# Where the compressed branch's scores and turned weights live in PSUM: a two-layer NSA and GLA trunk on one core

## The chip, the core and the metric

The kernel runs on one core of one Trainium2 chip. Its five engines are TensorE (PE, with its weight loads shown apart as PEld), VectorE (DVE), ScalarE (ACT), GpSimd (POOL) and SyncE (SP), which issues the transfers. The metric is the device time of one execution in microseconds (us), the median over several runs.

## The reference

The reference runs two layers over a sequence of 512 rows of width 1024. In each layer a normalised input is projected by one wide matrix; from the parts two branches are made, a sparse attention of eight heads in two groups and a gated linear attention, which are mixed by gates and projected back. The part that matters here is the attention of one head. It has three branches over the same queries: compressed keys (31 of them, of blocks of 32 rows), selected blocks, and a window.

```
def _masked_softmax(s, mask):
    s = jnp.where(mask, s.astype(jnp.float32), -jnp.inf)
    m = jnp.max(s, axis=-1, keepdims=True)
    ...
    return e / jnp.maximum(jnp.sum(e, axis=-1, keepdims=True), 1e-30)

s_c = jnp.einsum('bqghd,bgjd->bghqj', qn, k_cmp) * scale
p_c = _masked_softmax(s_c, cmp_end[None, :] <= t[:, None])
o_c = jnp.einsum('bghqj,bgjd->bqghd', p_c.astype(v_cmp.dtype), v_cmp)
...
o_s = jnp.einsum('bghqkl,bgqkld->bqghd', p_s.astype(v_sel.dtype), v_sel)
...
o_w = jnp.einsum('bghqk,bkgd->bqghd', p_w.astype(vwin.dtype), vwin)
return gt[..., 0:1] * o_c + gt[..., 1:2] * o_s + gt[..., 2:3] * o_w
```

With 512 rows there are eight blocks, so all blocks are selected and the window spans the sequence; selection and window differ in their keys and values alone.

## The kernel before

The work of a layer is laid out by hand for TensorE; for the other engines the order comes from a scheduler, and each engine runs its instructions in that order. Accumulators live in the eight banks of PSUM, given out by four pools: three banks `mm` for the projections, two `s` and two `t` for scores and transposes, one `o` for the attention's output (line 84). A bank is given again when its last reader on VectorE or ScalarE is through. The program fixes at build time which bank each tile gets.

A projection (`fm`, L164) takes one bank of `mm` and fills it in eight steps of three matmuls (`split3`, L160 to L162), each 128 by 512: a weight is split into a high and a low part, and so are the activations. Its epilogue on ScalarE and VectorE (for instance L436 and L438, or L595) reads the bank. The weights come by DMA into `raw`; ScalarE casts the high part (L145) and VectorE subtracts it for the low part (L146).

During the attention the projections still to be done wait in a queue. `fill(us)` works off as many projection steps as the credit given allows; `need(name)` works until a certain one is done. So the projections fill the gaps of the attention steps on TensorE, which would have nothing to do while VectorE and ScalarE do a softmax.

The attention goes over four pairs of heads p (0 to 3, here also called the first to the fourth pair). Each pair has five steps in the list `steps`: one compressed step and four steps `attn_steps`, for two halves of the queries (ip) times two branches (br). Each is a generator, and `go(n)` carries step n to its next `yield`. The compressed step, `cmp_steps`, has three stages. First the scores: a mask and four small matmuls into one bank (L733, L736), read by VectorE at L740 (the extreme) and L743 (the difference), then exponent, sum, and the scaled weights at L751. Then the turn: four transposes (L755) into one bank, read by ScalarE (L757) and VectorE (L758). Last the product with the values (L761, L762) into the bank `o`, in which the attention steps accumulate theirs (L841) until VectorE reads it at L846.

An attention step makes scores for two blocks of 128 queries. A unit is one such call of `scores`: two matmuls into one bank for each of two head groups (L800), two banks in all, both of one pool, `s` or `t` by turns. VectorE masks them and finds the extreme (L813), ScalarE takes the exponent (L815), VectorE scales (L817, L818) and transposes in blocks of 32 (L778); over DRAM (L783, L786) they come back as `PT` for L841.

The loop that sets the order on TensorE goes over the twenty steps, with m the place in a pair and four gaps of projections for each:

```
for n in range(len(steps)):
    m = n % 5
    f4 = FILL[m]
    ...
    go(n)
    ...
    fill(f4[0])
    if m == 1:
        go(n - 1)
    fill(f4[1])
```

At m = 1 `go(n - 1)` is the turn of the same pair.

Of the kernel before, what the change touches and what calls it, by code (L numbers as in the profile page):

```python
# [64 lines left out]
def trunk(ctx, tc, x, wpk, sp, gvec, cs, wa, out):  # L65
# [23 lines left out]
    def new(pl, shape=(128, 512), dt=F32, tag=None, bufs=None):  # L89
        cnt[0] += 1  # L90
        kw = {} if bufs is None else {"bufs": bufs}
        return sb[pl].tile(list(shape), dt, tag=tag or pl, name=f"{tag or pl}_{cnt[0]}", **kw)

    def ps(tag):
        cnt[0] += 1
        return psp[tag].tile([128, 512], F32, tag=tag, name=f"ps_{tag}_{cnt[0]}")
# [4 lines left out]
    mm, tp = nc.tensor.matmul, nc.tensor.transpose  # L101
# [169 lines left out]
    for l in range(L):  # L271
# [20 lines left out]
        def fill(us):  # L292
            credit[0] += us
            while credit[0] > 0.3 and queue:
                credit[0] -= step(*queue[0])
# [9 lines left out]
        def need(name):  # L305
            while name not in done:
                step(*queue[0])
# [421 lines left out]

        def cmp_steps(p):  # L730
            qn = PR[p][0]
            c = ps("s")[:, 0:256]
            mm(c, ident_b, pmask.rearrange("p i g j -> p (i g j)"), start=True, stop=False,  # L733
               skip_group_check=True)
            for i in range(4):
                mm(c[:, i * 64:(i + 1) * 64], qn[:, i * 128:(i + 1) * 128], kbd, start=False, stop=True,  # L736
                   skip_group_check=True)
            c3 = c.rearrange("p (a j) -> p a j", j=32)
            mx = new("sm", (128, 8), tag="mx8")
            V.tensor_reduce(mx, c3, axis=X, op=OP.min)  # L740
            pc = new("g")
            pc3 = pc[:, 0:256].rearrange("p (a j) -> p a j", j=32)
            V.tensor_sub(pc3, mx.unsqueeze(2).to_broadcast([128, 8, 32]), c3)  # L743
            A.activation(pc[:, 0:256], pc[:, 0:256], AF.Exp)
            sm = new("sm", (128, 8), tag="sm8")
            V.tensor_reduce(sm, pc3, axis=X, op=OP.add)
            rc = new("sm", (128, 4, 2), tag="rc8")
            V.reciprocal(sm, sm)
            V.tensor_mul(rc, gt[:, :, 3 * p:3 * p + 13:12], sm.rearrange("p (i g) -> p i g", g=2))
            V.tensor_scalar(rc[:, 0], rc[:, 0], valid, None, op0=OP.mult)  # L750
            V.tensor_mul(pc3, pc3, rc.rearrange("p i g -> p (i g)").unsqueeze(2).to_broadcast([128, 8, 32]))  # L751
            yield
            bk = ps("t")
            for i in range(4):
                tp(bk[0:64, i * 128:(i + 1) * 128], pc[:, i * 64:(i + 1) * 64], ident)  # L755
            pcT = new("p", dt=F32R)
            A.copy(pcT[0:64], bk[0:64])  # L757
            V.tensor_sub(pcT[64:128], bk[0:64], pcT[0:64].bitcast(F32))  # L758
            yield
            acc = PR[p][3] = ps("o")  # L760
            mm(acc, vbd[0], pcT, start=True, stop=False, skip_group_check=True)  # L761
            mm(acc, vbd[1], pcT, start=False, stop=False, skip_group_check=True)  # L762
            yield
# [90 lines left out]
        for p in range(4):  # L854
            steps.append((p, cmp_steps, ()))
            steps += [(p, attn_steps, (ip, br)) for ip in range(2) for br in range(2)]
        live = [f(p, *a) for p, f, a in steps]

        def go(n):
            if 0 <= n < len(steps):  # L860
                next(live[n])
# [19 lines left out]
# [3 lines that stand above are left out]
            if m == 0:  # L884
                need(f"q{steps[n][0]}")
            if m == 4:
                need(f"nz{steps[n][0]}")
            go(n)
            if m == 3:
                go(n - 5)  # L890
                go(n - 4)
            fill(f4[0])
            if m == 1:
                go(n - 1)
            fill(f4[1])
            if m != 0:
                go(n)
                fill(f4[2])
            if m == 3:
                go(n - 3)  # L900
            if m == 4:
                go(n - 3)
                go(n - 2)
            fill(f4[3])
# [126 lines left out]
```

## Time and profile before

| | us |
|---|---|
| median of 3 runs | 830.52 (827.52 to 830.93) |
| profiled execution | 832.5, span 830.4 |
| TensorE busy | 790.9, 95% of the span |
| VectorE busy | 557.5, 67% |
| ScalarE busy | 354.4, 43% |
| GpSimd busy | 99.5, 12% |
| granted TensorE clock, mean | 0.993 |

Busy time is the time in which an engine had an instruction in work, without the instructions that only wait or issue. Shares are over the whole span, and stages differ: what an engine waits for has to be looked up in the stage in question. Start times are from the span's start. The attention of the first layer runs from about 150 to 320 us, that of the second from about 553 to 723 us.

### The profile page before, as it was taken

Reading aid. Unit: us, or ns where it says so; the run is one execution under the profiler, and the core shown is the slowest. Engines: PE = TensorE matmul, PEld = TensorE weight load, DVE = VectorE, ACT = ScalarE, POOL = GpSimd, SP = SyncE. Lnnn points to the kernel's source line nnn. Section 1 sums busy time; section 2 is a strip of 40 time slices with the busy share of each in tenths; the row PEclk is TensorE's granted clock in tenths of the full one; section 3 lists DMA queues with packets and bytes.
Section 4 is the critical chain, followed back from the end, with each engine's and each line's share of the span. In section 5 each row is a group of like instructions: output and inputs, shape, how many; then the busy total and the mean of one; then the engine's idle time right before and its main releaser. Section 6 shows DMA issues by size and latency. Waiting matters only on the chain. (4 is left out here: it accounts for less than half of the span.)

```text
span 830.4 us, 12007 instructions
## 1 busy us (share of the span) xinstructions
PE 790.9 (95%) x4250; PEld 648.0 (78%) x4250; DVE 557.5 (67%) x1272; ACT 354.4 (43%) x727; POOL 99.5 (12%) x118
## 2 busy tenths in 40 slices
PE   3999999998989999999999999999898999999996
PEld 3888788786868787888888878887776787778886
DVE  5653749898978863655564366589988888356322
ACT  3591136554444433443256413555544544344211
POOL 3100023000001002221010001321000100022100
PEclk9999999999999999999999999999999999999999
DMA  8432214367476575556246112234756666745222
GB/s 289 158 125 77 69 55 123 110 189 211 144 224 214 180 226 143 161 166 214 77 140 216 52 55 73 79 112 145 219 183 201 198 190 208 205 141 168 85 102 76
DMA packets 54555, 124.55 MB, mean 150 GB/s; under 512 B 6592, under 2 KB 23520, under 8 KB 54496
## 3 DMA queue, kind: packets, MB, share of 16 engines
q1 hardware_dynamic: 54496, 123.79, 47.6%
q8 instruction: 33, 0.54, 0.3%
q14 instruction: 26, 0.21, 0.1%
HBM read 95.46 MB, written 25.17 MB: 145 GB/s over the span
## 5 line engine op out<-in xcount | busy, mean ns | idle before, releaser
L160 PE MATMUL ps_mm<-hT,hl 128*128 128x512 f32 x544 | 219.1, 403 | 0.0
L161 PE MATMUL ps_mm<-hT,hl 128*128 128x512 f32 x544 | 213.9, 393 | 0.0
L162 PE MATMUL ps_mm<-hT,hl 128*128 128x512 f32 x544 | 213.5, 392 | 0.0
L145 ACT CAST hl<-raw 128x1024 fp32r<-128x1024 f32 (+3 forms) x110 | 100.4, 915 | 159.7 <-PE ps_mm L161 104.5
L146 DVE TENSOR_TENSOR hl<-raw,hl 128x1024 fp32r<-128x1024 f32 (+3 forms) x109 | 119.5, 1098 | 52.5 <-ACT hl L145 43.6
L160 PEld LDWEIGHTS ps_mm<-hT,hl 128*128 128x128 f32 x544 | 103.4, 190 | 23.3 <-issue 3.1
L162 PEld LDWEIGHTS ps_mm<-hT,hl 128*128 128x128 f32 x544 | 103.1, 190 | 22.5
L161 PEld LDWEIGHTS ps_mm<-hT,hl 128*128 128x128 f32 x544 | 103.5, 190 | 19.3
L815 ACT ACTIVATE g<-g,sx 128x128 f32<-128x128 f32 (+3 forms) x128 | 71.3, 558 | 80.3 <-DVE sx L813 71.6
L778 DVE STREAM_TRANSPOSE T<-g 128x256 f32<-128x256 f32 (+3 forms) x128 | 58.9, 492 | 0.7
L818 DVE TENSOR_SCALAR g<-g,sx,gt 128x128 f32<-128x128 f32 (+3 forms) x128 | 58.3, 469 | 1.5
L161 PE MATMUL ps_mm<-oT,hl 128*128 128x512 f32 x128 | 50.3, 393 | 1.7 <-POOL oT L849 1.7
L160 PE MATMUL ps_mm<-oT,hl 128*128 128x512 f32 x128 | 50.9, 397 | 0.0
L162 PE MATMUL ps_mm<-oT,hl 128*128 128x512 f32 x128 | 49.8, 389 | 0.0
L849 POOL TENSOR_TENSOR oT<-p,oT 128x512 fp32r<-128x512 f32 x8 | 13.6, 1696 | 254.6 <-ACT oT L848 254.6
L841 PE MATMUL ps_o<-PT,a 128*64 128x256 f32 (+1 forms) x384 | 38.6, 348 | 1.8 <-DMA PT<-tp 1.8
L183 POOL TENSOR_TENSOR rs<-ms,mhalf 128x1 f32<-128x1 f32 (+1 forms) x24 | 18.0, 751 | 174.3 <-DVE ms L181 170.6
L869 POOL TENSOR_TENSOR p<-p,g 128x512 f32<-128x512 f32 x16 | 28.0, 1753 | 84.2 <-DVE p L868 72.7
L841 PEld LDWEIGHTS ps_o<-PT,a 128*64 128x64 f32 x384 | 25.4, 137 | 16.2 <-issue 6.8
L813 DVE CUSTOM_DVE_ANT_0 g<-ps_s,cmask 128x128 f32<-128x128 f32 (+3 forms) x64 | 29.2, 485 | 9.1 <-PE ps_s L800 9.1
L800 PE MATMUL ps_t<-a,a 128*128 128x256 f32 (+2 forms) x112 | 25.1, 337 | 9.1 <-DVE p L758 4.7
L162 PE MATMUL ps_mm<-hl,hT 128*128 128x296 f32 (+1 forms) x96 | 32.4, 338 | 1.4 <-DVE hT L213 1.4
(253 smaller groups left out, 1323.7 us busy)
## 6 DMA issues: line engine op xcount, KB each, us to landing
raw<-wpk SPq DMA_DIRECT2D x96, 512.0 KB, 3.8
tp<-T SPq DMA_DIRECT2D x16, 896.0 KB, 4.1
PT<-tp SPq DMA_DIRECT2D x64, 224.0 KB, 5.2
raw<-wpk SPq DMA_DIRECT2D x32, 256.0 KB, 3.0
tp<-T SPq DMA_DIRECT2D x16, 384.0 KB, 2.4
PT<-tp SPq DMA_DIRECT2D x64, 96.0 KB, 2.7
a<-wpk SPq DMA_DIRECT2D x16, 256.0 KB, 4.7
p<-x SPq DMA_DIRECT2D x16, 256.0 KB, 2.8
```

Of the source, the lines that this page charges most:

```text
L145: A.copy(H[:, :w], r[:, :w])
L146: (G if i == 1 else V).tensor_tensor(Lo[:, :w], r[:, :w], H[:, :w].bitcast(F32), op=OP.subtract)
L160: mm(o, w[0], h[0], start=first, stop=False)
L161: mm(o, w[0], h[1], start=False, stop=False)
L162: mm(o, w[1], h[0], start=False, stop=last)
L778: V.transpose(t[:, :, :, g], pps[g][:, :n * 128].rearrange("p (j b q) -> p b j q", j=n, b=4))
L800: mm(o[g][:, :ww], PR[p][1][g][:, i * 128:(i + 1) * 128], kn, start=(n == 0), stop=(n == 1))
L813: V.tensor_tensor_reduce(pp[:, :w], ob, cmask[:, 512 - w:512], 1.0, -3 * NEG, OP.add, OP.min, sx[:, 0:1])
L815: A.activation(pp[:, :w], pp[:, :w], AF.Exp, bias=sx[:, 0:1], scale=-1.0, accum_out=sx[:, 1:2])
L818: V.tensor_scalar(pp[:, :w], pp[:, :w], sx[:, 2:3], gt[:, i, h * 3 + 1 + br:h * 3 + 2 + br], op0=OP.mult, op1=OP.mult)
L841: mm(acc[g * 64:(g + 1) * 64, (i0 + 2) * 128 - w:(i0 + 2) * 128], vsw[j // 2][:, j % 2, c0:c0 + 64], m, start=False, stop=(br == 1 and j = ...
L869: G.tensor_tensor(t_, t_, y2[f], op=OP.add)
```

## The change

Two tiles change their pool and one stage its place. The compressed branch's scores take a bank of `mm` in place of `s`, its turned weights a bank of `mm` in place of `t`. The turn is called at m = 2, between the first two gaps, as `go(n - 2)`, where it was called at m = 1 as `go(n - 1)`. Nothing is computed in another way. The units alone take `s` and `t`.

```
@@ cmp_steps @@
-            c = ps("s")[:, 0:256]
+            c = ps("mm")[:, 0:256]
...
-            bk = ps("t")
+            bk = ps("mm")
@@ the loop over the steps @@
             fill(f4[0])
-            if m == 1:
-                go(n - 1)
+            if m == 2:
+                go(n - 2)
             fill(f4[1])
```

In the program's order on TensorE, first pair, the turn stood between two projection steps just before the second unit (the projection fills `ps_mm_1570`; `hT` are activations, `hl` weights, `a` on the right keys and queries, `g` the compressed weights):

```order
-L755 MATMUL ps_t_1574<-ident,g_1473 64x128 x4
 L160 MATMUL ps_mm_1570<-hT_113,hl_1410 128x512
 L161 MATMUL ps_mm_1570<-hT_115,hl_1410 128x512
 L162 MATMUL ps_mm_1570<-hT_113,hl_1411 128x512
-L800 MATMUL ps_t_1585<-a_1176,a_1310 128x256
-L800 MATMUL ps_t_1585<-a_1177,a_1310 128x256
-L800 MATMUL ps_t_1586<-a_1184,a_1313 128x256
-L800 MATMUL ps_t_1586<-a_1185,a_1313 128x256
+L800 MATMUL ps_t_1577<-a_1176,a_1310 128x256
+L800 MATMUL ps_t_1577<-a_1177,a_1310 128x256
+L800 MATMUL ps_t_1578<-a_1184,a_1313 128x256
+L800 MATMUL ps_t_1578<-a_1185,a_1313 128x256
```

The unit follows without the turn before it; only its tile numbers differ. The turn's new place on TensorE is eighteen matmuls further on, within the same projection:

```order
 L161 MATMUL ps_mm_1570<-hT_116,hl_1410 128x512
 L162 MATMUL ps_mm_1570<-hT_114,hl_1411 128x512
+L755 MATMUL ps_mm_1622<-ident,g_1473 64x128 x4
 L160 MATMUL ps_mm_1570<-hT_114,hl_1410 128x512
 L161 MATMUL ps_mm_1570<-hT_116,hl_1410 128x512
```

Its tile is now one of `mm`. On VectorE, in the same pair, the reader of the turn (L758) and an epilogue of a projection (L438) change places with the work of the units (`p_1549` and `p_1555` belong to the next queries' rotation, `T` is a block transpose's result):

```order
 L509 TENSOR_TENSOR p_1549<-p_1549,cst 128x512
-L818 TENSOR_SCALAR g_1598<-g_1598,sx_1597,gt_148 128x256
+L758 TENSOR_TENSOR p_1627<-ps_mm_1622,p_1627 64x512
 L512 TENSOR_TENSOR p_1555<-p_1555,p_1549 128x512
-L778 STREAM_TRANSPOSE T_301_1541<-g_1598 128x4x2x32
+L438 SCALAR_TENSOR_TENSOR oT_1635<-th_1633,ps_mm_1570 128x512
 L813 ISA g_1644,sx_1643<-ps_s_1637,cmask 128x256
 L813 ISA sx_1643 128x1
+L548 TENSOR_TENSOR a_1558<-p_1555,a_1558 64x512
+L548 TENSOR_TENSOR a_1561<-p_1555,a_1561 64x512
```

L758 stands behind the second unit's work where it stood ahead of it, and L438 ahead of the third unit's first read.

## Rows read from the trace of the kernel before

**Rows 1.** The page, busy time of each engine.

```profile
PE 790.9 (95%) x4250; PEld 648.0 (78%) x4250; DVE 557.5 (67%) x1272; ACT 354.4 (43%) x727; POOL 99.5 (12%) x118
```

**Rows 2.** Waits of TensorE: who waited for whom, us in total, times, longest.

```profile
PE ps_t L800 <- DVE p L758: 4.7, 2, 2.4
PE ps_t L800 <- DVE sx L813: 4.4, 4, 1.7
PE ps_t L755 <- DVE sx L817: 4.2, 2, 2.1
```

**Rows 3.** Timeline of TensorE, rows with a wait: start, length, instruction, idle before.

```profile
159.03 0.51 PE L800 MATMUL ps_t<-a,a 128*128 128x256 f32 x2 [1.68 <-DVE sx L813]
...
192.89 0.60 PE L755 MATMUL ps_t<-ident,g 128*64 128x128 f32 x4 [2.09 <-DVE sx L817]
...
201.10 0.51 PE L800 MATMUL ps_t<-a,a 128*128 128x256 f32 x2 [0.52 <-DVE sx L813]
...
234.97 0.75 PE L800 MATMUL ps_t<-a,a 128*128 128x256 f32 x2 [2.35 <-DVE p L758]
...
597.08 0.60 PE L755 MATMUL ps_t<-ident,g 128*64 128x128 f32 x4 [2.09 <-DVE sx L817]
```

**Rows 4.** Windows around waits: length, busy by engine, granted clock, DMA share, GB/s.

```profile
190.00:200.00 10.00, 7.91 (x33) 6.31 (x32) 8.44 (x37) 3.96 (x14) 0.24 (x1) 0.83 0.74 212
...
235.00:240.00 5.00, 5.00 (x16) 4.09 (x17) 3.66 (x11) 1.10 (x4) 0.00 (x0) 0.66 0.57 156
...
593.00:603.00 10.00, 7.91 (x42) 6.46 (x40) 9.50 (x39) 3.90 (x15) 1.30 (x1) 1.00 0.82 229
...
633.00:643.00 10.00, 7.53 (x30) 5.79 (x29) 8.15 (x33) 4.17 (x14) 0.00 (x0) 0.83 0.81 252
```

**Rows 5.** Windows of the attention stage, same columns; VectorE's busy time is the third.

```profile
150.00:192.90 42.90, 39.14 (x197) 31.86 (x196) 41.88 (x123) 22.47 (x55) 3.89 (x3) 1.00 0.55 171
192.90:235.00 42.10, 39.13 (x206) 31.04 (x206) 36.96 (x115) 20.37 (x52) 1.56 (x1) 0.96 0.62 186
...
192.70:211.40 18.70, 17.99 (x95) 14.28 (x96) 14.71 (x52) 7.33 (x22) 0.00 (x0) 0.91 0.57 154
...
597.00:614.00 17.00, 16.39 (x95) 13.04 (x96) 14.47 (x51) 7.12 (x21) 0.00 (x0) 1.00 0.60 169
```

**Rows 6.** Timeline of VectorE, the readers that the prediction names.

```profile
192.31 0.43 DVE L751 TENSOR_TENSOR g<-g,rc 128x256 f32<-128x256 f32 x1
...
210.66 0.66 DVE L846 SCALAR_TENSOR_TENSOR p<-ps_o,oT 128x512 f32<-128x512 f32 x1
...
228.46 0.39 DVE L743 TENSOR_TENSOR g<-mx,ps_s 128x256 f32<-128x256 f32 x1
...
266.12 0.42 DVE L743 TENSOR_TENSOR g<-mx,ps_s 128x256 f32<-128x256 f32 x1
...
613.26 0.66 DVE L846 SCALAR_TENSOR_TENSOR p<-ps_o,oT 128x512 f32<-128x512 f32 x1
```

**Rows 7.** Timeline of TensorE, the places at which the prediction compares.

```profile
198.81 0.39 PE L160 MATMUL ps_mm<-hT,hl 128*128 128x512 f32 x1
...
213.29 0.39 PE L761 MATMUL ps_o<-p,vbd 128*128 128x512 f32 x1
...
231.44 0.48 PE L160 MATMUL ps_mm<-hT,hl 128*128 128x512 f32 x1
...
271.94 0.48 PE L160 MATMUL ps_mm<-hT,hl 128*128 128x512 f32 x1
...
284.15 1.73 PE L841 MATMUL ps_o<-PT,a 128*64 128x256 f32 x16 [1.11 <-DMA PT<-tp]
...
615.89 0.39 PE L761 MATMUL ps_o<-p,vbd 128*128 128x512 f32 x1
```

**Rows 8.** Timeline of ScalarE in the first pair: a cast and a tanh.

```profile
163.47 1.05 ACT L145 CAST hl<-raw 128x1024 fp32r<-128x1024 f32 x1 [1.48 <-issue]
...
165.71 0.60 ACT L436 ACTIVATE th<-ps_mm 128x512 f32<-128x512 f32 x1
```

## The prediction

> **What bounds the kernel now.** Read the page's busy times first: TensorE works in 790.9 us of a span of 830.4 us [rows 1], so only its idle time and its clock can be won. The list of waits by engine, kept to TensorE, says which idle time the change can touch. Three of its rows name lines of the attention stage that wait for VectorE, together 4.7 + 4.4 + 4.2 = 13.3 us in eight waits [rows 2]. A larger row belongs to the kernel's start, which the change leaves as it is.
>
> The timeline of TensorE places them. In the first layer four waits stop it: 1.68, 2.09, 0.52 and 2.35 us, sum 6.64; the second layer repeats them, 2.09 shown [rows 3], and has the remaining 13.3 - 6.64 = 6.66. In three of the four the second head group of a small unit (L800, 256 columns, two banks of t) waits for a bank of t. The other bank is held by the turned weights of the compressed branch: they take a bank of t at L755 and give it back only when VectorE comes to L758. The fourth (192.89) is the turn itself, which waits for the weights that VectorE finishes at L751, at 192.31 + 0.43 = 192.74 [rows 6].
>
> A wait can also cost clock. The windows show a granted clock of 0.83 over 10 us around the first 2.09 us wait, 0.66 over 5 us after the 2.35 us wait and 0.83 over 10 us after its twin in the second layer: engine idle, then a stretch at 1.2 GHz instead of 2.4. Each loses 1.7 us (10 x 0.17, 5 x 0.34). The second layer's 2.09 us wait left the clock at 1.00 [rows 4]. So the waits are worth 13.3 + 3 x 1.7 = 18.4 us at most.
>
> Last look at the engine waited for. VectorE is busy 41.88 of 42.90 us while the first head pair runs, and 36.96 of 42.10 in the next stretch [rows 5]. It is as full as TensorE, so a wait that goes can come back as another.
>
> **The change part by part.** No instruction is added or removed; matrix columns and vector elements stay the same. (a) The compressed scores leave s and the turned weights leave t for the three banks mm of the projections. The four banks s and t then serve only the units, each in the two banks of the unit before last, whose reads are long done. The tightest place is the second pair: there the last read of those banks now stands just ahead of L751 in VectorE's order, so it is done before the turn, and the turn precedes the unit by two groups of matmuls. The three waits of L800 have no bank to wait for: 1.68 + 0.52 + 2.35 = 4.55 us in the first layer, the same in the second.
>
> (b) The turn moves from the gap before the small unit to the middle of the next step, one gap later. In the second pair it then stands at the place of the row at 198.81 [rows 7]. TensorE gets there, with its own 0.35 us of transposes still to come and with 1.68 + 2.09 + 1.7 less behind it, at 198.81 - 0.35 - 5.47 = 192.99. L751 is now ordered two small instructions later, about 0.45 us: 193.2. The wait falls from 2.09 to 0.3 us (bounds: 0, and 2.09 if VectorE slips as much as TensorE gains). Taken: 0.3 a layer.
>
> After 201.10 the lead in the first layer is 5.47 + 0.52 = 5.99 us; after 234.97 it is 8.34, with the clock 10.04. In the second layer there is one clock loss: 6.66 + 1.7 = 8.36.
>
> What is late next, place by place, since each is read by an engine that works in order:
>
> First, the compressed outputs of pair 2 (L761) go into the single bank o, and wait until L846 has read pair 1 out of it. Before, L846 ended at 210.66 + 0.66 = 211.32 and L761 began at 213.29 [rows 6, 7]. With the lead, TensorE is there at 213.29 - 5.99 = 207.30. From L751 to L846 VectorE was busy 14.71 of 18.70 us [rows 5], so it can be at most 4.0 earlier: 207.3, a tie. If it came no earlier, the wait would be 4.0. Part of its idle time is the way over ScalarE and back, which stays, and the first pair's order now puts the swish (L438) ahead of the scores' L813, behind a ScalarE tanh that follows a cast begun at 163.47, 1.05 long, and 0.60 for the tanh [rows 8]: VectorE stands up to 1 us, and the scores, key casts and transposes queue behind. I take 1.5 us. Second layer: 615.89 - 4.29 = 611.60 wanted, L846 ended at 613.26 + 0.66 = 613.92, VectorE had 17.00 - 14.47 = 2.53 us to give: 0 to 2.3, taken 1.2.
>
> Second, the projections' banks. In pairs 3 and 4 the projection after next gets the bank of the compressed scores and waits for L743. L743 ended at 228.85 and 266.54; the bank is wanted (231.44 - 0.36) - 5.99 = 225.1 and (271.94 - 0.36) - 10.04 = 261.5 [rows 6, 7]. If VectorE were no earlier: 3.7 and 5.0 us. I expect it 3 to 4 and 5 us earlier, since it idles where TensorE stood (5.1 us in 192.90 to 235.00): taken 0, upper bound 8.7 a layer.
>
> Third, the transposed weights come back by DMA. One L841 already waits 1.11 us [rows 7]; their transposes are VectorE's, and SyncE issues the reload behind weight loads that wait for VectorE's splits. If VectorE gains less than TensorE this grows, by up to some 3 us; with luck it vanishes, -1.1. Taken +0.5 a layer. The weights' splits keep their order on VectorE beside the units and are hidden behind the two projections loaded ahead.
>
> Sum: 13.3 + 5.1 = 18.4 won; 0.6 + 2.7 + 0 + 1.0 = 4.3 given back; net 14.1. The profiled execution took 832.5 us, 2.0 above the median of the three runs, 830.52. So 832.5 - 14.1 = 818.4 for such an execution, and 816.4 as a median. I say 816.5.
>
> **The rivals.** *VectorE keeps most of it.* For it: from 150.00 to 235.00 VectorE works 41.88 + 36.96 = 78.84 of 85.00 us [rows 5], so with no idle time at all it would be 6.2 us earlier there, less than TensorE's 8.34; half of the idle time is chain latency, which leaves 3 us a layer. Against it: TensorE may run ahead by two units and one turn, and VectorE has room later. It gives 830.5 - 6 = 824.5.
>
> *The projections starve for a bank* (the other side). The scores of pairs 3 and 4 hold one of three mm banks until L743, the projections cycle through two, and TensorE stands before each second projection. If VectorE comes no earlier it is 3.7 + 5.0 = 8.7 us a layer, 17.4 in all, and each of the four waits is over 2 us, where three of four such waits above cost clock: 4 x 1.7 = 6.8. Then 24.2 replaces 18.4: 830.5 + 5.8 = 836.3. It decides from the point where the four waits average 18.4 / 4 - 1.7 = 2.9 us, that is, where L743 is less than about 1.5 us earlier than before. For it: in VectorE's order L743 stands behind four transposes of the pair before. Against: VectorE's 5.1 us of idle time ahead of it, which the earlier scores fill with work. The stretch with the 1.68 us wait kept a granted clock of 1.00 [rows 5], so short waits are no matter for the clock. The Trainium skill speaks against the change here: "TensorE: Matmul & The Clock Gate", section "A second HAM failure mode: psum-queue depth-cycling", says that TensorE's clock oscillates where matmul groups cycle through PSUM banks with many tiny idle gaps. By that page even short waits at the mm banks would put the 6.8 us on top; the rows at 1.00 do not bear it out for single short waits.
>
> *Nothing is won.* The four waits come back whole at L761 and at the turn (4.0 + 2.1 in the first layer), with their clock: 830.5.
>
> **How the numbers follow.** My forecast 0.63, its own range 813 (1 us given back) to 821 (9); VectorE keeps most 0.22; nothing 0.09; starving 0.06. The range goes from 811.5, the whole 18.4 won (812.1) and a little scatter, to 826, past the first rival's time. Faster by over 0.5% (4.2 us, about what a measurement here can tell from no change) are the first two cases but the tail of the second: 0.83. Within 0.5%: the third case, that tail and a part of the fourth: 0.12. Slower: 0.05.
>
> **What would show it.** Right: in the list of TensorE's waits the two rows of L800 and the row of L755 fall from 13.3 to under 1.5 us; an L761 row of 1 to 4 us for VectorE appears; the granted clock over the span rises to 0.995 or more; VectorE is over 90% busy from the second pair's start to the third's. Wrong: a row of L160 in mm waiting for L743, L758 or L438; an L841 row of over 4 us; L761 rows of 6 us or more, which would be the first rival; or new stretches under full clock after them.

## The result, and the profile after

The changed kernel takes 817.16 us, median of 4 runs (816.13 to 819.83), beside 830.11 for the kernel before on the same chip: ratio 0.9847, 95% interval 0.9825 to 0.9868. The prediction was 816.5. The profiled execution took 817.14 us with a span of 815.1, against 832.5 and 830.4.

First the page's busy time of each engine, which answers to [rows 1]:

```profile
PE 787.2 (97%) x4250; PEld 646.6 (79%) x4250; DVE 553.8 (68%) x1272; ACT 353.5 (43%) x727; POOL 99.9 (12%) x118
```

TensorE's instructions are the same in number and its busy time hardly moved (790.9 to 787.2); the span lost idle time and little else. The list of TensorE's waits between 150 and 730 us (who waited for whom, us in total, times, longest), after:

```profile
PE ps_o L841 <- DMA PT<-tp: 4.6, 3, 2.7
PE ps_mm L161 <- POOL oT L849: 1.7, 2, 0.8
```

and the row of the kernel before that answers to the first:

```profile
PE ps_o L841 <- DMA PT<-tp: 1.8, 2, 1.1
```

The three rows of [rows 2], 13.3 us, are gone whole. No wait at an mm bank came for them, and none of L761. What grew is the wait of L841 for transposed weights that come back by DMA: 1.8 to 4.6 us, in three pieces. The timeline of TensorE, after, with the second pair's turn and product with the values, the third pair's projection that takes the bank of the scores, and the three waits:

```profile
192.62 0.60 PE L755 MATMUL ps_mm<-ident,g 128*64 128x128 f32 x4
...
206.99 0.39 PE L761 MATMUL ps_o<-p,vbd 128*128 128x512 f32 x1
...
224.53 0.39 PE L160 MATMUL ps_mm<-hT,hl 128*128 128x512 f32 x1
...
234.29 1.73 PE L841 MATMUL ps_o<-PT,a 128*64 128x256 f32 x16
238.76 2.48 PE L841 MATMUL ps_o<-PT,a 128*64 128x256 f32 x16 [2.74 <-DMA PT<-tp]
...
596.73 1.73 PE L841 MATMUL ps_o<-PT,a 128*64 128x256 f32 x16 [0.49 <-DMA PT<-tp]
...
634.63 1.73 PE L841 MATMUL ps_o<-PT,a 128*64 128x256 f32 x16 [1.35 <-DMA PT<-tp]
```

The L841 that waited before, at 284.15 [rows 7], waits no longer; the new 2.74 us belong to the last step of the second pair, a pair earlier in the program. VectorE's rows that answer to [rows 6], after:

```profile
191.83 0.42 DVE L751 TENSOR_TENSOR g<-g,rc 128x256 f32<-128x256 f32 x1
...
205.96 0.65 DVE L846 SCALAR_TENSOR_TENSOR p<-ps_o,oT 128x512 f32<-128x512 f32 x1
...
223.81 0.38 DVE L743 TENSOR_TENSOR g<-mx,ps_mm 128x256 f32<-128x256 f32 x1
...
229.47 1.18 DVE L146 TENSOR_TENSOR hl<-raw,hl 128x1024 fp32r<-128x1024 f32 x1
...
259.94 0.42 DVE L743 TENSOR_TENSOR g<-mx,ps_mm 128x256 f32<-128x256 f32 x1
```

VectorE ran 4.7 us earlier at L846 (210.66 to 205.96), 4.65 at the third pair's L743 and 6.2 at the fourth's. TensorE ran 6.3 us earlier at L761 (213.29 to 206.99), 6.55 at the third pair's bank (231.44 - 0.36 = 231.08 to 224.53) and 6.2 at the fourth's: VectorE followed it, at most 1.9 us short. The windows, after (length, busy by engine, granted clock, DMA share, GB/s), to be read against [rows 4, 5]:

```profile
150.00:192.90 42.90, 42.90 (x218) 35.46 (x217) 41.85 (x128) 23.59 (x59) 3.90 (x3) 1.00 0.59 176
192.90:235.00 42.10, 42.09 (x233) 33.84 (x233) 39.77 (x124) 21.42 (x55) 1.55 (x1) 1.00 0.67 200
190.00:200.00 10.00, 9.99 (x61) 7.78 (x61) 9.47 (x45) 5.32 (x19) 0.00 (x0) 1.00 0.87 251
...
236.00:246.00 10.00, 7.26 (x35) 5.59 (x34) 7.83 (x21) 2.87 (x6) 1.81 (x1) 0.83 0.64 203
...
633.00:643.00 10.00, 8.65 (x51) 6.85 (x48) 9.21 (x26) 4.50 (x10) 2.15 (x1) 1.00 0.64 212
```

TensorE stands for 0.01 us in the first 85 us of the stage; the VectorE column rose from 36.96 to 39.77 in the second window. Of the three stretches at 1.2 GHz of the kernel before none is left, and one is new: 0.83 over the 10 us around the 2.74 us wait, 1.7 us lost.

The sum of what the traces show: 13.3 won, 2.8 given back at L841 (4.6 - 1.8), three clock losses down to one, 2 x 1.7 = 3.4 won: 13.9. The medians moved by 13.0, the profiled executions by 15.4. The 1.5 us by which the profiled ones differ from the sum are in no wait row. They lie in the attention, half in each layer: from the first scores to the wait for L849 TensorE takes 7.46 and 7.95 us less, where the rows and the clock give 6.7 and 7.2. A wait moves what follows it by more than its idle time: from the first pair's unit in t to the next projection step it is 2.41 us with the 1.68 us wait (156.96 to 159.37) and 0.47 without it (156.51 to 156.98), so 1.94 for 1.68. Seven waits fewer at some 0.2 us each would make up the rest, by estimate.

Why the reload is late is read from SyncE's queue (start, duration with the wait in it, transfer), after:

```profile
223.92 0.34 SPq L783 DMA_DIRECT2D tp<-T  x1
224.82 6.20 SPq L132 DMA_DIRECT2D raw<-wpk  x2
232.17 1.75 SPq L786 DMA_DIRECT2D PT<-tp  x4
...
621.54 6.19 SPq L132 DMA_DIRECT2D raw<-wpk  x2
627.84 1.85 SPq L786 DMA_DIRECT2D PT<-tp  x4
```

with the reload's wait in the first layer and the time from the write's issue to its landing,

```profile
SPq L786 <- DMA tp<-T: 1.1, 1, 1.1
```

```profile
tp<-T SPq DMA_DIRECT2D x1, 896.0 KB, 8.2
```

and the same stretch of the kernel before, with the L841 that uses that reload:

```profile
228.57 0.34 SPq L783 DMA_DIRECT2D tp<-T  x1
229.47 7.07 SPq L132 DMA_DIRECT2D raw<-wpk  x2
236.65 1.80 SPq L786 DMA_DIRECT2D PT<-tp  x4
```

```profile
245.01 3.25 PE L841 MATMUL ps_o<-PT,a 128*64 128x256 f32 x32
```

The queue has one order in both: the transposed weights are written (L783), two weight loads follow, of which the second stands for some 6 us (until 230.65, as the L146 shown above ends), and behind them the reload (L786). In the first layer of the changed kernel the queue was free at 231.01, and the write held the reload 1.1 us longer: it landed 8.2 us after its issue (7.4 before). In the second layer the write landed after 6.3 us, and the reload left when the queue was free (627.73). The first layer's reload was issued 4.5 us earlier than before, but TensorE's L841 group came 10.7 us earlier: it ran through from 245.01 before, and began at 234.29 and stood from 236.02 (238.76 - 2.74) after. The way over DRAM, which had slack, now sets the pace.

### The profile page after: what moved, and what is told of

The parts are those of the page before. It is cut to its first block, busy times and chain, and to the rows that moved or that the text cites. A ratio compares the mean times of both kernels' runs of the same rounds, so it can differ in the third digit from the quotient of the medians.

```text
span 815.1 us, 12017 instructions
## 1 busy us (share of the span) xinstructions
PE 787.2 (97%) x4250; PEld 646.6 (79%) x4250; DVE 553.8 (68%) x1272; ACT 353.5 (43%) x727; POOL 99.9 (12%) x118
## 5 line engine op out<-in xcount | busy, mean ns | idle before, releaser
L160 PE MATMUL ps_mm<-hT,hl 128*128 128x512 f32 x544 | 217.5, 400 | 0.0
L146 DVE TENSOR_TENSOR hl<-raw,hl 128x1024 fp32r<-128x1024 f32 (+3 forms) x109 | 119.2, 1095 | 51.2 <-ACT hl L145 46.0
L160 PEld LDWEIGHTS ps_mm<-hT,hl 128*128 128x128 f32 x544 | 102.3, 188 | 23.2 <-issue 3.1
L160 PE MATMUL ps_mm<-oT,hl 128*128 128x512 f32 x128 | 51.2, 400 | 0.0
L841 PE MATMUL ps_o<-PT,a 128*64 128x256 f32 (+1 forms) x384 | 39.8, 353 | 4.6 <-DMA PT<-tp 4.6
L849 POOL TENSOR_TENSOR oT<-p,oT 128x512 fp32r<-128x512 f32 x8 | 13.9, 1738 | 241.7 <-ACT oT L848 241.7
L841 PEld LDWEIGHTS ps_o<-PT,a 128*64 128x64 f32 x384 | 26.1, 138 | 19.2 <-issue 10.2
L162 PE MATMUL ps_mm<-hl,hT 128*128 128x296 f32 (+1 forms) x96 | 32.7, 341 | 1.4 <-DVE hT L213 1.4
L160 PE MATMUL ps_mm<-hl,hT 128*128 128x296 f32 (+1 forms) x96 | 33.1, 345 | 0.7 <-ACT hT L212 0.7
L161 PE MATMUL ps_mm<-hl,hT 128*128 128x296 f32 (+1 forms) x96 | 32.5, 338 | 0.0
```

Of the source, the lines that this page charges most:

```text
L146: (G if i == 1 else V).tensor_tensor(Lo[:, :w], r[:, :w], H[:, :w].bitcast(F32), op=OP.subtract)
L160: mm(o, w[0], h[0], start=first, stop=False)
L161: mm(o, w[0], h[1], start=False, stop=False)
L162: mm(o, w[1], h[0], start=False, stop=last)
L841: mm(acc[g * 64:(g + 1) * 64, (i0 + 2) * 128 - w:(i0 + 2) * 128], vsw[j // 2][:, j % 2, c0:c0 + 64], m, start=False, stop=(br == 1 and j = ...
L849: G.tensor_tensor(Lo, f_, H.bitcast(F32), op=OP.subtract)
```

## Experiments

All were timed against the kernel before on the same chip; its median was 829.79 to 830.82 us on the chips used, so runs on different chips are best compared by their ratios. Three theories were set against each other on where the gain is from (e1 to e3), then the new wait was followed (e4, e5, e8), and the place where the prediction saw the largest price (e7).

**e1: the banks without the move.** The turn at its old place, in mm.

```
-            if m == 2:
-                go(n - 2)
+            if m == 1:
+                go(n - 1)
```

> The scores and the turned weights in mm, the turn left where it was. Theory (each part takes its own waits): the two rows of L800, 4.55 us a layer, go with the banks; the turn's wait for L751 does not. TensorE comes to the second pair's turn 1.7 us earlier (the 1.68 us wait ahead of it is gone), VectorE, solidly busy there, at most 0.5 us, so that wait grows from 2.1 to about 3.3 us and keeps its clock loss in the first layer. Won 2 x 4.55 + 1.7 (the clock after the 2.35 us wait) - 2 x 1.2 = 8.4, some 1 given to L841: about 822.5 us. Rival 1 (the banks do it all, the turn waits only because TensorE was stopped elsewhere): 817, no L755 row. Rival 2 (the move does it all): 828 to 830, with the L800 waits turned into an L755 wait of 4 us or more.

823.60 us; ratio 0.9925 (0.9908 to 0.9941). The L800 rows are gone and the turn's wait has grown, in both layers, as the theory had it. TensorE's timeline of e1 and the window after the first wait:

```profile
191.28 0.60 PE L755 MATMUL ps_mm<-ident,g 128*64 128x128 f32 x4 [3.37 <-DVE g L751]
...
591.16 0.60 PE L755 MATMUL ps_mm<-ident,g 128*64 128x128 f32 x4 [3.12 <-ACT g L815]
```

```profile
189.00:199.00 10.00, 7.72 (x33) 6.49 (x34) 7.61 (x36) 3.93 (x14) 1.17 (x1) 0.83 0.78 223
```

The banks alone win 6.2 us: part of what is removed in front of the turn is paid again at the turn, with its clock, and L841 waits 4.3 us in place of 1.8. By the rows 13.3 - 6.5 - 2.5, and one clock loss less, 1.7: 6.0.

**e2: the move without the banks.** The turn late, but in t, and the scores in s.

```
-            c = ps("mm")[:, 0:256]
+            c = ps("s")[:, 0:256]
...
-            bk = ps("mm")
+            bk = ps("t")
```

> The turn one gap later, scores in s and turned weights in t as in the kernel before. Theory (each part takes its own waits): the turn's wait (4.2 us in two) goes, with its clock loss of 1.7 us; the turned weights still hold one of the two banks of t until L758, so the small units of t still alternate in a single bank and wait for L813 and L758: 9.1 us stay, some of them at another unit, with their two clock losses. Won 4.2 + 1.7, perhaps 1 to 3 of it eaten by longer L800 waits: 825 to 828 us. Rival 1 (the banks do it all): 829 to 831. Rival 2 (the move does it all): 817 and no L800 row over 1 us.

820.68 us; ratio 0.9889 (0.9867 to 0.9910), better than the theory's 825 to 828. The waits that I had left standing went too, except one in each layer. TensorE's timeline of e2 and the window around the first wait:

```profile
198.21 0.52 PE L800 MATMUL ps_t<-a,a 128*128 128x256 f32 x2 [2.97 <-DVE sx L813]
...
596.61 0.50 PE L800 MATMUL ps_t<-a,a 128*128 128x256 f32 x2 [2.96 <-DVE sx L813]
```

```profile
195.00:205.00 10.00, 7.03 (x40) 5.18 (x40) 6.81 (x25) 3.61 (x12) 0.00 (x0) 0.83 0.89 252
```

In the first pair the unit comes ahead of the turn and finds both banks of t, so its 1.68 us go; no unit of pair 3 waits for L758 any more either. Only in the second pair do both head groups of a small unit share one bank. By the rows 13.3 - 6.2 (5.9 at L800, 0.3 at L755), 0.9 less at L841 (1.8 to 0.9) and one clock loss less, 1.7: 9.7, measured 9.1. So the move is worth more by itself than the banks (the intervals of the ratios just touch), and each removes a part that the other leaves: rivals 1 and 2 of both runs fall.

**e3: the scores back in s,** the turned weights in mm and late.

```
-            c = ps("mm")[:, 0:256]
+            c = ps("s")[:, 0:256]
```

> As the changed kernel, but the compressed scores in s again; the turned weights in mm and later. Theory (t's bank is what costs; s had no wait in the kernel before): same as the changed kernel within 1.5 us, 816 to 818.5, no new wait of L800 on L743. Rival (the scores' bank counts too): the second group of the unit after the scores waits for L743 in s, 1 us or more in pairs 2 to 4 of each layer, 821 to 825 us.

814.81 us; ratio 0.9822 (0.9805 to 0.9840). Neither held as it stood: the rival's wait for L743 is there, 0.69 us in each layer, and yet the median lies below the changed kernel's, though the intervals overlap. TensorE's timeline, the window and SyncE's queue of e3:

```profile
223.19 0.47 PE L800 MATMUL ps_s<-a,a 128*128 128x256 f32 x2 [0.69 <-DVE g L743]
237.43 1.74 PE L841 MATMUL ps_o<-PT,a 128*64 128x256 f32 x16 [1.74 <-DMA PT<-tp]
```

```profile
235.00:245.00 10.00, 8.26 (x52) 6.47 (x49) 8.97 (x26) 4.40 (x10) 2.05 (x1) 1.00 0.67 216
```

```profile
223.67 6.20 SPq L132 DMA_DIRECT2D raw<-wpk  x2
229.97 1.80 SPq L786 DMA_DIRECT2D PT<-tp  x4
```

The same L841 waits 1.74 us in place of 2.74, and the clock stays at 1.00. L841's waits fall from 4.6 to 2.8, one clock loss goes, and 1.4 come at L743: 2.1 us by the rows, 2.4 by the medians. Here the write landed after 7.0 us in place of 8.2, and the reload left as soon as the queue was free; whether the place of the scores has to do with that is not shown. Of the change's two banks, then, only that of the turned weights was needed.

**e4: one weight load behind the reload.** ug4's load is made to issue after the reload that L841 waits for; TensorE's order is unchanged.

```
-        dma(r[:, :w], src)
+        with tc.issue_after(back[-13]) if n == 'ug4' and len(back) >= 13 else nullcontext(): dma(r[:, :w], src)
```

> The changed kernel with one weight load of each layer (ug4, 128x512) issued behind the second pair's last reload of transposed weights in place of ahead of it. Theory (the new L841 waits, 2.74 us in the first layer with a clock loss of 1.7 and 1.35 in the second, come from SyncE's queue: the reload stands behind a load that waits 5.8 us for a buffer): the 1.35 goes whole; in the first layer the write of the weights landed only 1.1 us after that load was issued, so 1.1 to 2.7 goes, and the clock loss with it if under 1 us is left. 811.5 to 815 us. Rival 1 (VectorE's transposes and the transfers set it, not the queue): both waits stay within 0.5 us, 816.5 to 817.5. Rival 2 (the load that is put back comes late): a wait of TensorE for hl at L160, 818 or more.

813.26 us; ratio 0.9809 (0.9788 to 0.9830), inside the theory's range. SyncE's queue and TensorE's timeline of e4:

```profile
223.18 0.34 SPq L783 DMA_DIRECT2D tp<-T  x1
224.09 0.35 SPq L132 DMA_DIRECT2D raw<-wpk  x1
229.79 2.71 SPq L786 DMA_DIRECT2D PT<-tp  x4
```

```profile
236.29 1.74 PE L841 MATMUL ps_o<-PT,a 128*64 128x256 f32 x16 [1.10 <-DMA PT<-tp]
...
630.02 1.73 PE L841 MATMUL ps_o<-PT,a 128*64 128x256 f32 x16 [1.11 <-DMA PT<-tp]
```

The first wait falls from 2.74 to 1.10 us and its clock loss goes (0.83 to 1.00 in the 10 us around it); no wait for hl at L160 came. In the second layer only 0.24 of the 1.35 us went, where I expected all: the reload now waits for the write itself, not for the queue. The write landed after 6.6 and 6.8 us. In the first layer it had let the reload go last in the changed kernel too, so what was won there is a write that landed 1.6 us sooner, for which no run shows the reason; in the second layer, where the queue had let it go last, leaving the queue earlier won 0.3 us. The order of the loads is worth 3.9 us by the medians (the intervals just touch), but not through the place in the queue alone, as the theory had it.

**e5: both weight loads behind the reload.**

```
+        with tc.issue_after(back[{'mgg4': -9, 'ug4': -13}[n]]) if n in ('mgg4', 'ug4') and len(back) > 12 else nullcontext(): dma(r[:, :w], src)
```

> The changed kernel with both weight loads (mgg4, 128x1024, and ug4) issued behind that reload. Theory (in e4 the write of the turned weights, 0.9 MB, still took over 5 us to land beside the 0.5 MB load issued just after it, and the reload waits for it): without a load beside it the write lands earlier, the reload is issued at about 227 in place of 229.8 us, both L841 waits of e4 (1.1 us each) go: 811 to 812.5 us, if the load of mgg4, now some 10 us later, is still in time. Rival: it is not; its split is late, and TensorE waits for hl at L160 by 1 us or more in each layer, or a later L841 waits instead: 813.5 to 818.

811.39 us; ratio 0.9775 (0.9755 to 0.9795), as expected in size, but not by the expected way. SyncE's queue, its wait and TensorE's timeline of e5:

```profile
223.43 0.34 SPq L783 DMA_DIRECT2D tp<-T  x1
230.20 1.73 SPq L786 DMA_DIRECT2D PT<-tp  x4
```

```profile
SPq L786 <- DMA tp<-T: 6.4, 1, 6.4
```

```profile
236.25 1.73 PE L841 MATMUL ps_o<-PT,a 128*64 128x256 f32 x16 [0.49 <-DMA PT<-tp]
```

The write lands no sooner without the load beside it (6.7 us from issue to landing, 6.6 in e4): that part of the theory falls, and why 0.9 MB take so long here stays open. The wait falls to less than half all the same, 1.10 to 0.49 and 1.11 to 0.38 in the second layer. The reload's four parts take 1.73 us to issue in place of 2.71 (2.33 in the second layer of e4), so that, counted from each layer's first scores, the last is out 0.8 and 0.9 us sooner. In the second layer that covers what the wait lost; in the first TensorE also came 0.3 us later. What held the parts apart in e4 was not tried. Its interval overlaps that of e4.

**e6: e3 and e4 together,** the two edits above.

> The scores back in s (as e3) and ug4's load behind the reload (as e4). Theory (e3 beat the changed kernel only since its L841 wait was 1.74 us in place of 2.74 and cost no clock, and it pays 0.69 us a layer for L743 at the small unit in s): with the L841 waits cut in both, the scores in s are no better than in mm: 812.5 to 814, with the L743 waits there. Rival (s is the better place, VectorE's order is shorter with it): as much better than e4 as e3 was than the changed kernel, 810 to 811.5.

813.49 us; ratio 0.9794 (0.9775 to 0.9813), level with e4, as the theory had it. No L841 waits here; the small unit waits for L743, 0.48 and 0.69 us. So the place of the scores is worth nothing that these runs can tell, and e3's lead came through L841.

**e7: VectorE late at the bank o.** The reader of o done five times in the first pair of each layer.

```
-                V.scalar_tensor_tensor(f_, acc, 0.5, PR[p][2], op0=OP.mult, op1=OP.mult)
+                for _ in range(1 if p else 5): V.scalar_tensor_tensor(f_, acc, 0.5, PR[p][2], op0=OP.mult, op1=OP.mult)
```

> The changed kernel with VectorE's reader of the bank o (L846) done five times over in the first pair of each layer: four more of 0.6 us, 2.4 us in all, ahead of the second pair's L761; nothing else is changed. Theory (the bank o was met with little to spare, 0.38 us in the first layer by L846's end at 206.61 against L761 at 206.99, 0.89 in the second): L761 waits 2.0 and 1.5 us, 3.5 more in all, and since VectorE falls behind the turns and reloads too, up to 2 us follow: 820.5 to 823. Rival 1 (VectorE has room, the tie was none): no L761 row, 817 to 818. Rival 2 (VectorE paces the stage): the full 4.8 and clock on top, 823 to 826.

822.61 us; ratio 0.9913 (0.9896 to 0.9930): the theory's total, with other terms. TensorE's timeline of e7, VectorE's last reading, and the window:

```profile
211.42 0.76 PE L761 MATMUL ps_o<-p,vbd 128*128 128x512 f32 x1 [4.67 <-DVE sx L817]
...
609.86 0.47 PE L761 MATMUL ps_o<-p,vbd 128*128 128x512 f32 x1 [4.67 <-DVE sx L817]
```

```profile
210.59 0.68 DVE L846 SCALAR_TENSOR_TENSOR p<-ps_o,oT 128x512 f32<-128x512 f32 x1
```

```profile
206.00:216.00 10.00, 5.33 (x18) 4.04 (x17) 8.27 (x17) 3.26 (x7) 1.28 (x1) 0.83 0.33 105
```

The scheduler spread the readings among other instructions, so the last one ended at 211.27, 4.66 us after 206.61, not 2.4 (4.85 counted from the first scores, which this execution reached 0.19 sooner). L761 began 0.15 us behind that end, 4.62 later by the same count, though the profile names L817, the next instruction of VectorE. But for a margin of some 0.2 us the bank o passes a delay on one for one. Two waits of 4.67 make 9.3, with two clock losses 12.7; but L841 then waits nowhere, and its 4.6 and one clock loss come back: 12.7 - 6.3 = 6.4, measured 5.4. The two waits are alternatives here: what holds TensorE at o gives the reload its time.

**e8: the kernel before with e5's edit alone.**

> The kernel before with the edit of e5 alone (both weight loads behind the second pair's last reload), to see whether that order was worth anything before the banks were changed. Theory (the reload became late only because TensorE came earlier; in the kernel before no L841 of the second pair waits for it): nothing won, 828.5 to 831 us, all rows of L800 and L755 as before. Rival (the weight loads crowd the stage whatever TensorE does, and e5's gain has nothing to do with the lead): 5 us won as from the changed kernel to e5, 824 to 826.

830.32 us; ratio 1.0001 (0.9989 to 1.0013). In the list of TensorE's waits in e8 the three rows of [rows 2] stand with the same figures, and L841 with:

```profile
PE ps_o L841 <- DMA PT<-tp: 1.7, 2, 1.2
```

Nothing moved. The queue's order cost nothing until the bank waits were gone; the same edit that won 5.8 us behind the change (817.16 to 811.39) wins none ahead of it.

**e9: the scores in s, and both loads behind the reload.**

> The three edits that helped together: turned weights in mm and later, scores in s, both weight loads behind the reload. Theory (e6 stood level with e4, so the place of the scores is worth nothing once the reload is in time, and s costs its waits for L743, 0.5 to 0.7 us a layer): level with e5 within 1.5 us, 811 to 813. Rival (what e3 won adds to what e5 won): 808.5 to 810.

813.16 us; ratio 0.9793 (0.9779 to 0.9806): level with e5 within the intervals, though its median is 1.8 us higher, where the theory allowed 1.5; the rival falls. The waits for L743 are there, 1.0 us in two, those of L841 sum to 0.9. The lowest median is that of e5, the change with two loads issued later: 2.2% below the kernel before, where the change is 1.5% below it.

## Why the prediction was right, point by point

**What is won** came as the rows said: the eight waits, 13.3 us, went to nothing and the three clock losses with them. e1 and e2 show that neither half of the change does it: banks alone 6.2 us, move alone 9.1, both 13.0.

**The turn** was priced at 0.3 us a layer and cost nothing. TensorE was there at 192.62 (192.99 worked out), and L751 ended at 192.25, where I had taken 193.2: VectorE got there half a microsecond earlier than before, not half later, in spite of the order.

**The bank o (L761)** was priced at 1.5 + 1.2 us and cost nothing. This step failed in VectorE's part. TensorE came at 206.99 (207.30 worked out); L846 ended at 206.61, earlier than the earliest that I allowed, 207.3. I had split VectorE's 3.99 us of idle time between 192.7 and 211.4 [rows 5] into waiting for TensorE, which goes, and latency, which stays. From L751's end to L846's end VectorE now takes 14.36 us where it took 18.58. The two stretches, before and after (VectorE's busy time is the third):

```profile
192.74:211.32 18.58, 17.91 (x95) 14.20 (x96) 14.59 (x52) 7.25 (x21) 0.00 (x0) 0.91 0.58 155
```

```profile
192.25:206.61 14.36, 14.35 (x86) 11.29 (x85) 13.59 (x49) 6.45 (x19) 0.00 (x0) 1.00 0.69 189
```

The idle time fell from 3.99 to 0.77, so 3.2 of it had been waiting; another 1.0 us is work that no longer stands in this stretch, and the stretch began 0.5 us sooner. My bound of 4.0 had kept the work and the start fixed; VectorE came 4.7 earlier. And the delay that I expected from L438 behind a tanh did not come: L438 began at 164.18 without a wait. e7 shows that the place is as critical as I took it; it was met by 0.4 us.

**The banks mm** were priced at nothing, rightly and narrowly: L743 ended at 224.19 and TensorE came for the bank at 224.53 (225.1 worked out). In the fourth pair there was room: 260.36 against 265.40 (261.5 worked out, without the stop at L841). The rival of starving projections fell: no wait at an mm bank came up in the stage. The rule set beside it, of the Trainium skill ("TensorE: Matmul & The Clock Gate", section "A second HAM failure mode: psum-queue depth-cycling"), that the clock oscillates where small idle times between matmul groups come often, is not put to the test by any run here. The nearest row is e3's single wait of 0.69 us at a bank of s, which left the granted clock at 1.00 from 190 to 235 us.

**The reload (L841)** is the term that was mis-sized: +0.5 us a layer taken, with "up to some 3 us" as its bound, against 2.8 in all and a clock loss of 1.7. I had named one cause (SyncE issues the reload behind loads that wait for VectorE), not the time that the write before it takes to land, 8.2 us in the first layer, and I looked for the wait at the L841 that already waited, at 284.15. It came at another, which had had some slack, at the point where TensorE's lead is largest. And no term held the clock that such a wait costs.

So 4.3 us were given back by the prediction and 4.5 by the trace (2.8 + 1.7), but not at the same places: 3.3 of mine lay on VectorE, all of the real ones on the reload's way over DRAM. That the median came within 0.7 us is in part two errors that offset each other. The signs named beforehand say the same: the bank rows at nothing, the clock at 0.997 and VectorE busy for 94% of the second stretch (39.77 of 42.10) as forecast; the L761 row missing, and an L841 row of 4.6, which was listed as a sign of being wrong.

## What to carry to other kernels

When waits are removed from a full engine, list every consumer of a transfer in the stretch where the lead builds up, with its landing time against the new need, and not only those that wait already: e8 and e5 show one queue order worth nothing before and 5.8 us after. An engine's idle time that is waiting for the engine you speed up goes along with it: 3.2 of 3.99 us of VectorE's between L751 and L846. Where a neighbour has no idle time it doesn't follow: in the stretch where VectorE was 98% busy over 43 us L751 ended only 0.5 us sooner, and TensorE would have stood there (3.37 us in e1) but for the turn's later place. And what is won at several places isn't a sum: holding TensorE at o for 9.3 us removed 4.6 us of waits elsewhere.

## What the hardware showed that I had not expected

The clock's price did not grow with the wait. Around waits of 2.36 us (kernel before, second layer), 2.74 (the change), 2.97 (e2), 3.37 (e1) and 4.67 us (e7) the granted clock was 0.83 over 10 us each time, 1.7 us; waits of 1.10, 1.68 and 1.74 us left it at 1.00, and of the two 2.09 us waits one cost it and one did not [rows 3, 4]. Here a wait of 2.74 us cost 4.4 and one of 1.74 cost 1.74, so a microsecond off the one was worth more than its length, which is how e3 and e4 won.

A write of 0.9 MB took 6.6 us to land with a weight load issued behind it, 6.7 without one and 8.2 in the changed kernel with two, of which one came late, so what slows it is not that one neighbour. In the kernel before it was 7.4, in e3 7.0; what sets it stays open.
